# Latent attention on row halves: single banks for the maxima, denominators in a score bank, four query buffers, every engine in source order

## The chip, the cores and the metric

The kernel runs on one core of a Trainium2 chip. A core has five engines with a queue each: TensorE (PE, matmuls, with its weight loads shown as PEld), VectorE (DVE), ScalarE (ACT), GpSimd (POOL) and SyncE (SP), which issues most DMAs here. TensorE writes into PSUM, eight banks of 128 partitions by 512 fp32 words; the engines work otherwise on SBUF, which DMAs fill from and empty to HBM. The metric is the time of one execution on the device in microseconds (us); lower is better.

## The reference, cut to what matters

Two layers over 1024 latent tokens and 256 context tokens of width 1024: windowed grouped attention first, then multi-head latent attention, then a final RMSNorm. The change lies in the second layer.

```python
def latent_attention(hx, hc, w_in, q_norm, w_uq, kv_norm, w_ukv, w_out, cos, sin, need_ctx):
    scale = (B_NOPE + B_ROPE) ** -0.5                     # 64 + 32
    def project(h):
        cq, ckv, kr, g = jnp.split(h @ w_in, ...)
        q = (rms_norm(cq, q_norm) @ w_uq).reshape(b, n, B_HEADS, B_NOPE + B_ROPE)
        kv = (rms_norm(ckv, kv_norm) @ w_ukv).reshape(b, n, B_HEADS, B_NOPE + B_V)
        return q[..., :B_NOPE], q[..., B_NOPE:], kv[..., :B_NOPE], kr, kv[..., B_NOPE:], g
    ...
    def attend(qn, qr, kn, kr, v):
        s = (jnp.einsum("bqhd,bkhd->bhqk", qn, kn)
             + jnp.einsum("bqhd,bkd->bhqk", qr, kr)).astype(F32) * scale
        p = jax.nn.softmax(s, axis=-1).astype(v.dtype)
        return jnp.einsum("bhqk,bkhd->bqhd", p, v)
    ...
    yx = (ox * jax.nn.silu(gx)) @ w_out
...
x = x + gate_x[:, None] * yx
return rms_norm(x, final_g)
```

16 heads, 1024 queries, 1280 keys (context and latent), fp32 throughout.

## The kernel before

**Numbers and layout.** Matmul operands are split into a high part and a rest (`split`, L119: ScalarE copies the high part, another engine subtracts for the low part); `mm3` (L124) makes three matmuls of such pairs. Everything lives in two hand-laid arenas of SBUF, `R` (matmul operands) and `F` (fp32), addressed in KB per partition, and in the eight banks of `PB`.

**Units.** Attention runs over 16 units (`UnitB`): unit i is a pair of heads (i // 2) and a half of the queries (i % 2, 512 of them). The two heads of a pair lie in the two halves of the partitions, so their matmuls come in pairs on 64 rows each ("row halves"). Scores are computed with keys on partitions and queries on the free axis, in ten chunks of 128 keys. A softmax needs the maximum of each query first; since keys lie on partitions, the maxima are taken in a pass of their own with queries on partitions (`top`), from the high parts alone, and enter the scores as extra rows of the query operand.

**One unit.** In the loop over the ten chunks (L1491), `score(c)` makes ten matmuls into a bank pair (2 and 3, or 4 and 5), ScalarE takes the exponential of both banks into a buffer of a ring of six (`Er`, L1340), and POOL adds it to the denominators (L1343, L1345). Behind each score comes one piece of the next unit's maxima, `top(PIECES[c])`: four matmuls (or eight of half the size) into banks 0 and 1, and one reduce by VectorE over both (L1311, L1313). At c == 5 come the previous unit's denominators (`fin2`: matmuls with ones into bank 7, `fin3`: reciprocals in the bank, products) and the first five chunks of PV, which add up in bank 6; at the end the other five. Then `shift` reduces the pieces' maxima, transposes them on TensorE into bank 7 (L1318), and VectorE (L1320) and ScalarE (four small activations, L1327) write them into the next unit's query operand. Behind it stands filler work for later units: `make_K` (the keys of the next pair, in units 0, 2, ..., 12) or `make_V` (values of the next four heads, in units 3, 7, 11), through banks 0, 1 and 7.

**Buffers.** Queries have three buffers (`qbufs`): one for unit 0, two that alternate. `prep` loads a unit's queries by five DMAs. The normalised result of a unit is stored to `og_d`.

**Around it.** Ahead of the units, unit 0's maxima are interleaved with the last four gate tiles (`g_tile`). The output weights are loaded and split in 16 pieces (`wo_pieces`) that the unit loop takes one by one. Behind the units `out_tiles` multiplies eight tiles of 128 tokens with the output weights: at the top of its loop a tile's operand is split, then 48 matmuls in two halves, for each half VectorE multiplies by the gate and adds the residual (L1428, L1429) and ScalarE squares (L1430); POOL makes the norm's factor in three small steps (L1444 to L1446), and VectorE multiplies (L1457).

**What sets the order.** Inside `tc.manual_schedule(...)` the named engines keep the order of the source. Before, only TensorE is named (L1472); the other engines' queues, SP's DMAs included, are ordered by the framework's scheduler, which may bring later work forward. An engine works its queue strictly from the front.

## Time and profile before

| | us |
|---|---|
| median of 3 runs | 1663.95 (1663.37 to 1664.39) |
| the profiled execution, its own time | 1665.06 |
| its span | 1663.2 |

| engine | busy us | share |
|---|---|---|
| TensorE | 1565.0 | 94% |
| VectorE | 969.3 | 58% |
| POOL | 767.0 | 46% |
| ScalarE | 727.4 | 44% |

The attention units run from about 1004 to 1568 us of the span, the output stage from there to the end. A row of the timeline gives start, length, engine, line, operation, output and inputs, how many instructions are merged, and in brackets how long the engine stood idle before and what ended that. A row of the chain of waits gives start, length and what the end of the program waited for at that time. A row of windows gives for each engine the busy time and number of instructions in that stretch, then the granted TensorE clock, the DMA share and GB/s. A row by source line gives shortest, median and longest instruction in ns, and the start of the first and of the last.

### The profile page before, as it was taken

What the parts mean: (1) busy time and instruction counts of PE and PEld (TensorE: products, weight loads), DVE (VectorE), ACT (ScalarE), POOL (GpSimd) and SP (SyncE); (2) the same over time, 40 slices, a digit from 0 to 9 for tenths busy, and PEclk for the clock granted to TensorE, in tenths of its full rate; (3) what the DMA queues carried; (4) which work ended last, traced back from release to release, by engine and by line L of the source; (5) the groups of instructions that cost most, each with busy time, mean ns of one, the idle gap of its engine ahead of it and who ended that gap; (6) DMA issues with size and microseconds to landing.
All of it is one profiled execution on the core that took longest, in us unless ns stands there. A gap on an engine that the chain in (4) does not pass through costs nothing.

```text
span 1663.2 us, 24529 instructions
## 1 busy us (share of the span) xinstructions
PE 1565.0 (94%) x9026; PEld 1176.9 (71%) x9026; DVE 969.3 (58%) x1734; ACT 727.4 (44%) x1412; POOL 767.0 (46%) x711
## 2 busy tenths in 40 slices
PE   7899999989999999989999997999999999999898
PEld 3788888777888888879878884556555555655487
DVE  2676689547777777777251035544565456555354
ACT  3511222258777777775224214333434343333321
POOL 2653265235453334444174203655566557566500
PEclk8899999999999999999999998999999999999899
DMA  8445553663343222263048324011111111131141
GB/s 306 146 133 172 190 168 124 198 177 112 97 139 93 89 90 89 64 198 103 23 160 293 107 65 141 20 51 35 42 40 44 53 40 35 48 99 36 57 158 64
DMA packets 123697, 178.90 MB, mean 108 GB/s; under 512 B 11692, under 2 KB 71724, under 8 KB 123576
## 3 DMA queue, kind: packets, MB, share of 16 engines
q1 hardware_dynamic: 116296, 166.40, 31.6%
q10 hardware_dynamic: 7280, 10.92, 2.1%
q8 instruction: 71, 1.16, 0.3%
q14 instruction: 50, 0.41, 0.1%
HBM read 131.13 MB, written 46.15 MB: 107 GB/s over the span
## 4 chain that ended last, share of the span: by engine, by line
PE 72%; DVE 13%; issue 4%; ACT 4%; POOL 3%; DMA 3%; SPq 0%; POOLq 0%; DVEq 0%; ACTq 0%
PE PB L126 13%; PE PB L127 12%; PE PB L128 12%; DVE krF L1311 9%; PE PB L1352 8%; PE PB L1305 7%; PE PB L570 5%; PE PB L560 4%; PE PB L1338 3%; PE PB L533 2%; PE PB L534 2%; PE PB L1363 1%; ACT arena_r L1327 1%; DVE arena_f L344 1%; PE PB L674 1%
## 5 line engine op out<-in xcount | busy, mean ns | idle before, releaser
L126 PE MATMUL PB<-arena_r 128*128 128x512 f32 (+2 forms) x1312 | 479.3, 366 | 13.4 <-ACT arena_r L1327 9.3
L127 PE MATMUL PB<-arena_r 128*128 128x512 f32 (+2 forms) x1312 | 472.3, 360 | 3.1 <-POOL arena_r L727 2.2
L128 PE MATMUL PB<-arena_r 128*128 128x512 f32 (+2 forms) x1312 | 471.8, 360 | 0.2 <-DVE arena_r L122 0.2
L1345 POOL TENSOR_TENSOR arena_f<-arena_f 128x1024 f32<-128x1024 f32 x128 | 305.0, 2383 | 81.1 <-ACT arena_f L1340 72.7
L126 PEld LDWEIGHTS PB<-arena_r 128*128 128x128 f32 x1312 | 252.3, 192 | 60.5 <-ACT arena_r L1327 11.1
L127 PEld LDWEIGHTS PB<-arena_r 128*128 128x128 f32 x1312 | 252.2, 192 | 38.1 <-POOL arena_r L727 2.7
L128 PEld LDWEIGHTS PB<-arena_r 128*128 128x128 f32 x1312 | 251.9, 192 | 35.9 <-DVE arena_r L122 0.4
L1340 ACT ACTIVATE arena_f<-PB 128x1024 f32<-128x1024 f32 x160 | 164.1, 1026 | 226.0 <-PE PB L1338 222.8
L1311 DVE TENSOR_REDUCE krF<-PB 128x2 f32<-128x1024 f32 x132 | 158.9, 1209 | 127.1 <-PE PB L1305 126.9
L1338 PE MATMUL PB<-arena_r 64*128 64x512 f32 (+1 forms) x1600 | 222.4, 400 | 9.1 <-ACT arena_f L1340 5.5
L122 DVE TENSOR_TENSOR arena_r<-PB,arena_r 128x512 fp32r<-128x512 f32 (+2 forms) x215 | 140.4, 664 | 98.1 <-ACT arena_r L121 97.2
L1338 PEld LDWEIGHTS PB<-arena_r 64*128 64x128 f32 (+1 forms) x1600 | 153.6, 187 | 59.3 <-issue 14.1
L122 POOL TENSOR_TENSOR arena_r<-arena_f,arena_r 128x512 fp32r<-128x512 f32 x80 | 111.5, 1408 | 166.3 <-ACT arena_r L121 164.9
L540 DVE CUSTOM_DVE_ANT_0 arena_f<-PB,arena_f,small 128x256 f32<-128x256 f32 (+1 forms) x288 | 145.5, 524 | 32.3 <-PE PB L534 25.7
L121 ACT CAST arena_r<-PB 128x512 fp32r<-128x512 f32 (+2 forms) x215 | 120.3, 564 | 66.6 <-PE PB L560 39.6
L1352 PE MATMUL PB<-arena_f 128*64 128x512 f32 x640 | 147.3, 607 | 0.0
L1305 PE MATMUL PB<-arena_r 64*128 64x512 f32 (+1 forms) x768 | 116.8, 391 | 29.1 <-DVE krF L1311 25.5
L541 ACT ACTIVATE arena_f<-arena_f,small 128x640 f32<-128x640 f32 (+2 forms) x160 | 118.9, 744 | 27.8 <-DVE small L540 26.9
L570 PE MATMUL PB<-arena_r 128*128 128x512 f32 x336 | 120.7, 435 | 4.7 <-ACT arena_f L581 4.1
L1305 PEld LDWEIGHTS PB<-arena_r 64*128 64x128 f32 x768 | 61.3, 187 | 84.4 <-DVE krF L1311 71.6
L344 DVE SCALAR_TENSOR_TENSOR arena_f<-arena_f,small 128x512 f32<-128x512 f32 x98 | 116.3, 1232 | 4.8 <-DMA arena_f<-ada_w 4.5
L1343 POOL TENSOR_TENSOR arena_f<-arena_f 128x1024 f32<-128x1024 f32 x16 | 38.2, 2390 | 168.9 <-ACT arena_f L1340 128.2
(162 smaller groups left out, 1878.4 us busy)
## 6 DMA issues: line engine op xcount, KB each, us to landing
arena_r<-q_d SPq DMA_DIRECT2D x148, 128.0 KB, 2.8
arena_f<-ada_w SPq DMA_DIRECT2D x64, 256.0 KB, 3.3
arena_f<-a_w_in SPq DMA_DIRECT2D x40, 256.0 KB, 3.1
arena_f<-ada_w SPq DMA_DIRECT2D x16, 512.0 KB, 7.2
arena_f<-x SPq DMA_DIRECT2D x16, 512.0 KB, 4.4
q_d<-arena_f SPq DMA_DIRECT2D x16, 512.0 KB, 3.0
qn_d<-arena_f SPq DMA_DIRECT2D x16, 512.0 KB, 5.7
arena_r<-qn_d SPq DMA_DIRECT2D x16, 512.0 KB, 5.0
```

The source lines that it names most:

```text
L122: (lo_eng or nc.vector).tensor_sub(lo, src, hi.bitcast(F32))
L126: nc.tensor.matmul(o, ah, bh, start=first, stop=False)
L127: nc.tensor.matmul(o, al, bh, start=False, stop=False)
L128: nc.tensor.matmul(o, ah, bl, start=False, stop=last)
L540: nc.vector.tensor_tensor_reduce(o, S, mk, -A_SCALE, prev, ALU.add, ALU.min, mx)
L570: nc.tensor.matmul(self.pv, V[:, self.chunks[ci], self.g, :], PT[:, s], start=ci == 0 and s == 0, stop=ci == self.m - 1 and s == 1,)
L1305: nc.tensor.matmul(PB[:, bank + e, o : o + n], self.q[r, s, bs], k[r, 0, n0 : n0 + n], start=s == 0, stop=s == 2)
L1311: nc.vector.reduce_max(self.mxp[:, :, b, i], src, AX.X)
L1338: nc.tensor.matmul(PB[:, b + e, :], k[r, s, cs], q[r, sq], start=i == 0, stop=i == 4)
L1340: nc.scalar.activation(E, PB[:, b : b + 2, :], AF.Exp)
L1345: nc.gpsimd.tensor_add(acc, acc, E)
L1352: nc.tensor.matmul(PB[r, 6, :], Vq[:, c, h, :], E[:, e], start=c == 0, stop=c == NT - 1)
```

## The change

The maxima go through three banks (0, 1, 2) that are taken in turn; each piece takes two of them, one per head, and each bank has a reduce of its own. The score pairs move to banks 3 and 4, and 5 and 6; PV adds up in bank 7. The transposed maxima and the denominators go to bank 5 (`psd`), one of the score banks; ScalarE copies the denominators to SBUF (over the sums that they were made from), and the reciprocals run there. The fillers use banks 0 to 2. `shift` is cut into `turn` (reduce and transpose) and `shift` (the writes, with the engine for each half named), and `fin3` into `fin3` and `fin4`. Queries have four buffers: one each for unit 0 and unit 1, two that alternate. Output-weight splits have their low part on POOL; in the last unit VectorE makes the additions after the fifth chunk. A small exponential is put ahead of the first unit. Every engine now keeps the order of the source, and the calls in the source are moved accordingly. `out_tiles` itself is not changed.

```diff
-    qbufs = [r_at(o, 4, 512) for o in (10, 32, 40)]
+    qbufs = [r_at(o, 4, 512) for o in (10, 48, 32, 40)]
...
-    fillb = Banks(0, 1, 7)
+    fillb = Banks(0, 1, 2)
+    topb = Banks(0, 1, 2)
+    psd = PB[:, 5, :]
...
-    WoB = [r_at(o, 2, 1024) for o in (48, 56, 80, 88, 96, 104, 64, 72)]
+    WoB = [r_at(o, 2, 1024) for o in (56, 80, 88, 96, 104, 48, 64, 72)]
...
-            self.q = qbufs[0 if i == 0 else 1 + (i - 1) % 2]
+            self.q = qbufs[i if i < 2 else 2 + i % 2]
...
-        def top(self, piece, bank=0):
+        def top(self, piece, banks=None):
+            banks = banks or (topb(), topb())
...
-            src = PB[:, bank : bank + 2, 0 : n * len(piece)]
-            if len(piece) == 1:
-                nc.vector.reduce_max(self.mxp[:, :, b, i], src, AX.X)
-            else:
-                nc.vector.reduce_max(self.mxp[:, :, b : b + 2, i], src.rearrange("p e (b n) -> p e b n", b=2), AX.X)
-
-        def shift(self):
+            for e, bank in enumerate(banks):
+                if len(piece) == 1:
+                    nc.vector.reduce_max(self.mxp[:, e, b : b + 1, i], bank[:, 0:n], AX.X)
+                else:
+                    nc.vector.reduce_max(self.mxp[:, e, b : b + 2, i], shp(bank, 2, 256), AX.X)
+
+        def turn(self):
             nc.vector.reduce_max(shp(self.mx, 2, 64)[:, :, 32:36], self.mxp, AX.X, negate=True)
-            pm = PB[:, 7, 0:128]
-            nc.tensor.transpose(pm[0:100], self.mx[:, 0:100], ident)
...
+            nc.tensor.transpose(psd[0:100, 0:128], self.mx[:, 0:100], ident)
+
+        def shift(self, engs):
+            for r, eng in zip((slice(32, 36), slice(96, 100)), engs):
...
-            b = 2 + 2 * (c % 2)
+            b = 3 + 2 * (c % 2)
...
+            eng = nc.vector if self.i == NU - 1 and c > 4 else nc.gpsimd
             if c == 1:
-                nc.gpsimd.tensor_add(acc, self.E[0], E)
+                eng.tensor_add(acc, self.E[0], E)
...
             for e, r in enumerate(HALF):
-                nc.tensor.matmul(PB[r, 7, :], ones, acc[:, e], start=True, stop=True)
+                nc.tensor.matmul(psd[r, :], ones, acc[:, e], start=True, stop=True)
+            self.rec = self.acc[:, 0:512]
+            nc.scalar.copy(self.rec, psd)
 
         def fin3(self, j):
             js = slice(256 * j, 256 * j + 256)
-            nc.vector.reciprocal(PB[:, 7, js], PB[:, 7, js])
-            nc.vector.tensor_mul(self.o[:, js], self.o[:, js], PB[:, 7, js])
-            if j:
-                nc.vector.tensor_mul(self.o, self.o, self.gt.bitcast(F32))
-                load(out=og_d[self.pair, :, self.ts], in_=self.o)
+            nc.vector.reciprocal(self.rec[:, js], self.rec[:, js])
+            nc.vector.tensor_mul(self.o[:, js], self.o[:, js], self.rec[:, js])
+
+        def fin4(self):
+            nc.vector.tensor_mul(self.o, self.o, self.gt.bitcast(F32))
+            load(out=og_d[self.pair, :, self.ts], in_=self.o)
...
-                split(WoB[k][:, 0, cs], WoB[k][:, 1, cs], st)
+                split(WoB[k][:, 0, cs], WoB[k][:, 1, cs], st, nc.gpsimd)
...
-    in_order = tc.manual_schedule(engines={mybir.EngineType.PE})
+    in_order = tc.manual_schedule()
...
-            units[0].top([(b, i)], 2 * i)
-        for _ in gs[b]:
-            pass
-    units[1].prep()
-    units[0].shift()
+            units[0].top([(b, i)], (PB[:, 2 * i, :], PB[:, 2 * i + 1, :]))
+        next(gs[b])
+        next(gs[b])
+        if b == 3:
+            units[0].turn()
+            units[0].shift((nc.vector, nc.vector))
+        next(gs[b])
+        if b == 1:
+            units[1].prep()
+    nc.scalar.activation(const[:, 1:2], const[:, 1:2], AF.Exp)
...
-        if nu and ui:
-            nu.prep()
+        nnu = units[ui + 2] if ui + 2 < NU else None
         for c in range(NT):
             if c == 5:
                 if pu:
                     pu.fin2()
+                u.PV(0, 5)
+                if pu:
                     pu.fin3(0)
-                    if nu is None:
-                        pu.fin3(1)
-                u.PV(0, 5)
+                if pu and nu is None:
+                    pu.fin3(1)
+                    pu.fin4()
...
-            if 0 < ui < 12 and (c == 3 or c == 8 and ui == 6) or ui in (12, 13) and c in (3, 8):
+            if 0 < ui < 12 and c == 2 or ui == 6 and c == 7 or ui in (12, 13) and c in (2, 7):
                 next(wo_fill, None)
...
+        if nnu:
+            nnu.prep()
         if nu is None:
-            out_fill = out_tiles(fetch_out(0))
-        if pu and nu:
-            pu.fin3(1)
+            nxt = fetch_out(0)
         u.PV(5, NT)
-        u.fin()
         if nu:
-            nu.shift()
+            nu.turn()
+            if pu:
+                pu.fin3(1)
+            nu.shift((nc.vector, nc.scalar))
+            if pu:
+                pu.fin4()
             fill = make_K(u.pair + 1) if u.half == 0 and u.pair < 7 else iter(())
...
+        u.fin()
+    out_fill = out_tiles(nxt)
+    next(out_fill)
     next(out_fill)
     next(out_fill)
     units[-1].fin2()
     units[-1].fin3(0)
     units[-1].fin3(1)
+    units[-1].fin4()
```

More of the change, by code (lines that the diff above doesn't have):

```diff
@@ L1309, in top @@
[L1309 to L1327 removed]
+            b, i = piece[0]
```

36 lines of the change are left out of this document (16 added, 20 removed).

## The prediction

> **What bounds the kernel now.** I read the page first, then the last-ended chain of waits inside one attention unit, then the timeline around the stretches where TensorE stands still, and last the output stage.
>
> ```profile
> span 1663.2 us, 24529 instructions
> PE 1565.0 (94%) x9026; PEld 1176.9 (71%) x9026; DVE 969.3 (58%) x1734; ACT 727.4 (44%) x1412; POOL 767.0 (46%) x711
> PE 72%; DVE 13%; issue 4%; ACT 4%; POOL 3%; DMA 3%; SPq 0%; POOLq 0%; DVEq 0%; ACTq 0%
> ```
>
> TensorE carries 72% of the chain, VectorE 13%. VectorE's share comes from the attention units, where the chain alternates:
>
> ```profile
> 1281.34 1.24 DVE krF L1311
> ...
> 1282.62 0.75 PE PB L1305 x4
> ...
> 1284.68 0.75 PE PB L1305 x4
> ```
>
> ```profile
> 1281.14 1.31 PE L1338 MATMUL PB<-arena_r 64*128 64x512 f32 x10
> L1338 PE MATMUL PB<-arena_r x1600: 383/390/792, 1004.7 to 1560.8; 64*128 64x512 f32 x141, 36*128 36x512 f32 x37
> L1311 DVE TENSOR_REDUCE krF<-PB x132: 682/1226/1227, 976.0 to 1528.6; 128x2 f32<-128x1024 f32 x128, 128x2 f32<-128x512 f32 x4
> ```
>
> Each chunk of a unit runs a score (ten matmuls, L1338) and a maximum piece of the next unit (four matmuls, L1305, into banks 0 and 1) that one reduce over both banks empties (L1311). The next piece waits for that reduce. Pieces start at 1282.62 and 1284.68, a period of 2.06 us: 0.75 for the piece, 1.24 for the reduce, and gaps. What TensorE would need alone: ten score matmuls last 1.31 us with 0.39 for the last one, so a pair (the two row halves run together) takes (1.31 - 0.39) / 4 = 0.23; seven pairs are 1.61 us. So 0.45 us of each chunk is the reduce, not TensorE. That is the first bound.
>
> The second lies in the units' length. The transpose L1318 marks their boundaries:
>
> ```profile
> L1318 PE MATMUL PB<-ident,krF x16: 316/317/318, 1004.5 to 1535.0; 128*100 128x128 f32 x16
> 1365.71 0.32 PE L1318 MATMUL PB<-ident,krF 128*100 128x128 f32 x1
> 1396.88 0.32 PE L1318 MATMUL PB<-ident,krF 128*100 128x128 f32 x1
> 1430.58 0.32 PE L1318 MATMUL PB<-ident,krF 128*100 128x128 f32 x1
> 1467.95 0.32 PE L1318 MATMUL PB<-ident,krF 128*100 128x128 f32 x1
> ```
>
> Fifteen unit periods last 1535.0 - 1004.5 = 530.5 us. Three that nothing else disturbs are 31.17 (no filler), 33.70 (with a key filler L1263 behind the transpose) and 37.37 (with a value filler). Four, seven and three such periods would make 472.7 us, so with unit 0 in the place of one more, some 27 us are lost to disturbances:
>
> ```profile
> 1004.48 0.32 PE L1318 MATMUL PB<-ident,krF 128*100 128x128 f32 x1 [1.09 <-ACT arena_f L1146]
> 1017.96 5.74 DVE L122 TENSOR_TENSOR arena_r<-arena_f,arena_r 128x512 fp32r<-128x512 f32 x3
> 1024.88 1.22 PE L1305 MATMUL PB<-arena_r 64*128 64x256 f32 x8 [4.99 <-DVE krF L1311]
> 1048.87 0.50 PE L126 MATMUL PB<-arena_r 128*128 128x512 f32 x1 [1.93 <-ACT arena_r L1327]
> 1049.90:1053.30 3.40, 3.40 (x10) 2.61 (x9) 0.69 (x1) 0.59 (x1) 0.00 (x0) 0.51 0.00 0
> ```
>
> Unit 0 waits 4.99 us for a reduce behind output-weight splits that VectorE was given early; the filler at 1048.87 stands 1.93 us because bank 7 holds the transposed maxima until ScalarE's L1327 has read them, and the next 3.4 us run at a granted clock of 0.51.
>
> **The change part by part.**
>
> *Single banks for maxima.* A piece takes two of three banks in turn, with one reduce each. The trace has reduces of 512 columns at 0.68 us (the minimum of L1311; 1.23 for 1024), so two cost 1.36 in place of 1.23, 0.13 us more per chunk on VectorE. The first matmul of a piece needs the second reduce of the piece before last, and the second matmul needs the first reduce of the last piece. That one ends 0.62 (two pairs with their tail) + 0.05 + 0.68 = 1.35 us after its piece began; TensorE comes back after 1.61. So the chunk falls to 1.61 and VectorE, at 1.36 of it, is not the bound, by a margin of 0.26. Four of five chunks in a block were held, two blocks a unit: 8 x 0.45 = 3.6, and the last held piece of each block lasts 0.62 in place of the 0.75 quoted: 3.8 us per unit. Bounds: 2.8 if 0.1 of each wait stays, 4.1 if a pair takes 0.225.
>
> *Denominators in bank 5, fillers in banks 0 to 2.* The filler no longer shares a bank with the transposed maxima, so the 1.93 us and its slow clock go. The clean periods only lose the 3.8: 27.4, 29.9 and 33.6. (The key filler is 18 matmuls, 12 x 0.23 + 6 x 0.12 = 3.5 us, but its period is only 2.53 longer; the other 0.95 is the shift of the new maxima, for which a unit without filler waits and still will.) Copying the denominators out (L1368, as long as the copy L1356 of that shape, 0.58 below) and the reciprocal (1.76 below) lie beside the 4.46 us of PV matmuls; without that cover they would cost at least 2.3 a unit.
>
> *Unit 0 and the output weights.* The splits go to one per unit, low part on POOL, and unit 1's query has a buffer of its own, loaded two gate tiles earlier. Unit 0 becomes a clean unit without denominators: 27.4 - 1.0 for these, - 0.95 (its shift is hidden), + 1.4 for six gate matmuls moved behind its transpose: 26.8. The transpose itself comes 1.4 + 1.09 (the idle quoted) = 2.5 us earlier. POOL gets one split more a unit, half the size of an addition, beside nine additions of 2.4 us (7.27 for three, below): 23 us of 27.4, and the six exponential buffers cover its lag inside a unit.
>
> The fifteen periods: 4 x 27.4 + 7 x 29.9 + 3 x 33.6 + 26.8 = 446.5, against 530.5: **-84.0**, and -2.5 ahead of them.
>
> *Last unit.* Today the scheduler puts the first output tile's splits into ScalarE's queue amid the exponentials, and they wait for a load:
>
> ```profile
> 1537.22 5.72 PE L1338 MATMUL PB<-arena_r 36*128 36x512 f32 x41 [0.58 <-ACT arena_r L1327]
> 1542.88 1.08 PE L1363 MATMUL PB<-arena_f,small 128*64 128x512 f32 x4
> 1543.79 4.46 PE L1352 MATMUL PB<-arena_f 128*64 128x512 f32 x20
> ...
> 1556.92 1.04 ACT L121 CAST arena_r<-arena_r 128x1024 fp32r<-128x1024 f32 x1 [5.01 <-DMA arena_r<-og_d]
> 1557.99 1.22 DVE L122 TENSOR_TENSOR arena_r<-arena_r 128x1024 fp32r<-128x1024 f32 x1 [7.60 <-ACT arena_r L121]
> 1558.94 2.50 PE L1338 MATMUL PB<-arena_r 64*128 64x512 f32 x10 [5.53 <-ACT arena_f L1340]
> 1558.90:1565.40 6.50, 6.46 (x20) 2.72 (x22) 2.81 (x2) 3.00 (x3) 6.22 (x3) 0.50 0.52 148
> 1567.77 0.50 PE L126 MATMUL PB<-arena_r 128*128 128x512 f32 x1
> 1567.89 0.58 ACT L1356 COPY arena_f<-PB 128x512 f32<-128x512 f32 x1 [5.33 <-PE PB L1352]
> ```
>
> From 1542.88 to the first output matmul at 1567.77 are 24.9 us. In source order: 0.9 + 4.5, five chunks at (5.72 - 0.39) / 4.1 = 1.3 for 6.5, PV 4.5, then, in series, ScalarE's copy 0.58, its split 1.04 and VectorE's half 1.22 with gaps: 19.4. The stop of 3 us before the tile brings a slow clock, 1.7 to 3.4 us of half speed lost; I take 2.0. **-3.5** (bounds -5.5 and -2).
>
> *The output stage, in source order.* This is the part that costs. Today it is full:
>
> ```profile
> 1570.00:1600.00 30.00, 30.00 (x133) 23.92 (x132) 16.90 (x21) 5.73 (x12) 1.97 (x6) 1.00 0.36 114
> 1573.62 0.69 DVE L1428 TENSOR_TENSOR arena_f<-PB,arena_r 128x512 f32<-128x512 f32 x1 [11.08 <-PE PB L128]
> 1574.35 0.69 DVE L1429 TENSOR_TENSOR arena_f<-arena_f,arena_r 128x512 f32<-128x512 f32 x1
> 1574.95 1.76 DVE L1367 RECIPROCAL PB<-PB 128x256 f32<-128x256 f32 x1
> 1575.13 0.63 ACT L1430 ACTIVATE arena_f<-arena_f 128x512 bf16<-128x512 f32 x1 [6.66 <-DVE arena_f L1429]
> 1575.67 0.18 ACT L1430 ACTIVATION_READ_ACCUMULATOR arena_f<-arena_f 128x1 f32 x1
> ...
> 1579.53 0.69 DVE L1370 TENSOR_TENSOR arena_f<-arena_f,arena_r 128x512 f32<-128x512 f32 x1
> ```
>
> ```profile
> 1593.44 0.29 POOL L1444 TENSOR_TENSOR small<-small 128x1 f32<-128x1 f32 x1 [8.23 <-ACT arena_f L1430]
> ...
> 1594.09 0.55 POOL L1446 TENSOR_TENSOR small<-small 128x1 f32<-128x1 f32 x1
> 1594.68 1.41 DVE L1457 SCALAR_TENSOR_TENSOR arena_f<-arena_f,small 128x512 f32<-128x512 f32 x2 [1.00 <-POOL small L1446]
> ```
>
> because the scheduler splits tile n+1 while tile n multiplies. The source splits a tile at the top of its own loop, behind everything of the tile before; the compiled order of the changed kernel has on ScalarE both squares of a tile and then the cast of the next, and on VectorE the two final multiplies (L1463) and then the low half. At each of seven boundaries TensorE, done with tile n, waits for: VectorE's multiply and add (1573.62 to 1575.04) 1.42 and 0.1 before it, the square with its accumulator to 1575.85, 0.81; POOL's three small steps 1593.44 to 1594.64, 1.20, and 0.1; the two final multiplies 1.41; the low half 1.22 of which 0.08 overlaps; gaps 0.1. Sum 6.3 us; the high half (1.04) fits beside POOL. After stops of 5 to 6 us the trace shows half speed (granted clock 0.50) for 6.5 us of work at 1558.90; after the shorter 1.93 for 3.4 us. I take 5.2, which loses 2.6 (bounds 0 and 3.3). At the first boundary the last unit's denominators (1574.95 to 1580.22, 5.3 us of VectorE) stand ahead of the tile's own multiply. Counted from the tile's first half, twelve matmuls 2.75, the denominator matmuls 1.08 and the copy 0.58 let them begin at 4.5 and end at 9.8; the second half ends at 6.6, so 3.1 more. Together 7 x (6.3 + 2.6) + 3.1 = **+65.4** (bounds +47 and +70).
>
> *VectorE against POOL.* Where a denominator product read PSUM, it now reads two SBUF operands (L1373).
>
> ```profile
> 1542.58 7.27 POOL L1345 TENSOR_TENSOR arena_f<-arena_f 128x1024 f32<-128x1024 f32 x3
> 1548.57 1.83 DVE L1370 TENSOR_TENSOR arena_f<-arena_f,arena_r 128x512 f32<-128x512 f32 x1
> ```
>
> The one final product of today that met a running POOL addition took 1.83 us in place of 0.69: it ended 0.55 us after that addition. In the new order the second half's product stands ahead of the shift. It is asked for some 3.5 us into the PV block (reduces 1.36, reciprocal 1.76, small steps), the shift 4.46 + 0.3 into it, so a wait of up to 0.9 is hidden; a whole addition, 2.4, would delay the shift 1.5. With any phase as likely as any other that is a mean of 0.47 for 14 units, 6.6 us; a chain of additions that begins with the sixth exponential ends one about when the product is asked for, so I take +3 (bounds 0 and 14 x 1.5 = +21). [...]
>
> **Sum**: -2.5 - 84.0 - 3.5 + 65.4 + 3.0 = -21.6 us. The profiled execution took 1665.06 for a span of 1663.2 and was 1.1 above the median of the runs, 1663.95; the sum off the median gives 1642.3. Anything that moves the kernel before 974 us I take as zero within 2 us.
>
> **The rivals.**
>
> *A: the output stage keeps its overlap.* Then the 65.4 falls away save the 3.1: 1580. For it speaks only that a full stage is what the page shows now; against it the order of the two queues. 7%.
>
> *B: the maxima still hold the chunk.* If a piece waited for both reduces of the last one (0.62 + 0.05 + 0.60 + 0.68 + 0.04 = 1.99 us), the chunk would stay near 2.0 and 120 chunks would each give back 0.38 us: 46 us, 1688, slower than before. It decides from a chunk of about 1.8 us, where 22 us are given back. Against it: three banks leave each matmul only the older reduce. 11%.
>
> *C: the lock term is paid in full.* VectorE's product waits a whole POOL addition ahead of each shift, and the longer stop at the unit's end (1.93 us was enough for one slow stretch) costs clock in the five units without filler, 5 x 1.7: 1642.3 + 18 + 8.5 = 1669, a little slower than before. For it: POOL adds without a break there. Against it: the phase. 9%.
>
> *Main*: 73%, with an own range of 1622 to 1659 (chunks +-8, clock in the output stage -18 and +5, lock +10).
>
> **How the numbers follow.** The point is the main case, 1642.3. The 80% range takes in the main range and C: 1615 to 1669. What a measurement of this kernel can tell from no change is about 0.2%, 3.3 us: faster means below 1660.6. Main is faster in nearly all of its range (70 of 73), A always, C in 1 of 9: 0.78. Within 0.2%: 2 of main, 3 of C: 0.05. Slower: B, 5 of C and 1 of main: 0.17.
>
> **What would show it.** Right: transposes 27 to 28 us apart in units without filler; L1305 waiting for L1311 no more; slow clock gone between 1009 and 1160; in the output stage seven TensorE stops of about 6 us ended by VectorE's L122, each followed by half-speed matmuls, the first one longer. Wrong: a chunk of 1.8 us or more, stops of less than 4 us in the output stage, or L1373 lasting over 2 us in most units with the shift late behind it.

## The result, and the profile after

| | kernel before | changed kernel |
|---|---|---|
| median, measured together | 1663.66 us | 1641.47 us (1639.62 to 1646.49) |
| ratio | | 0.9873 [0.985, 0.9896] |
| span of the profiled execution | 1663.2 us | 1639.5 us |
| the fifteen unit periods | 530.5 us | 451.2 us |
| first output matmul to the end of the span | 95.5 us | 158.6 us |

The changed kernel is faster by 22.2 us, 1.3%; the interval of the ratio lies below 1. The forecast was 1642.3 with a range of 1615 to 1669. The page of the changed kernel: span, busy times, shares of the chain of waits, and the groups of the output matmuls with TensorE's idle time before them.

```profile
span 1639.5 us, 24729 instructions
...
PE 1541.3 (94%) x9026; PEld 1196.6 (73%) x9026; DVE 1008.0 (61%) x1886; ACT 733.7 (45%) x1425; POOL 776.3 (47%) x722
...
PE 79%; DVE 6%; issue 5%; POOL 4%; ACT 3%; DMA 2%; POOLq 0%; DVEq 0%; SPq 0%; ACTq 0%
...
L126 PE MATMUL PB<-arena_r 128*128 128x512 f32 (+2 forms) x1312 | 484.0, 369 | 30.8 <-ACT arena_r L121 27.6
L127 PE MATMUL PB<-arena_r 128*128 128x512 f32 (+2 forms) x1312 | 478.0, 365 | 18.7 <-DVE arena_r L122 15.6
```

VectorE's share of the chain fell from 13% to 6%: no piece waits for a reduce any more. In their place stand waits of the output tiles for their own split: TensorE's idle time is 30.8 us ahead of L126, most of it until ScalarE's half is done, and 18.7 ahead of L127, most of it until VectorE's half is done. In the kernel before these two were 13.4 and 3.1.

The timeline of the changed kernel in a block of a unit:

```profile
1281.04 0.63 PE L1305 MATMUL PB<-arena_r 64*128 64x512 f32 x4
1281.71 1.29 DVE L1311 TENSOR_REDUCE krF<-PB 128x1 f32<-128x512 f32 x2 [0.33 <-PE PB L1305]
...
1282.65 0.63 PE L1305 MATMUL PB<-arena_r 64*128 64x512 f32 x4
```

Pieces start at 1281.04 and 1282.65, so a chunk takes 1.61 us, and now VectorE waits for the pieces (0.33), not the pieces for VectorE. The transposes that mark the units, first their group (count, shortest, median and longest in ns, first and last start), then three of them on the timeline:

```profile
L1317 PE MATMUL PB<-ident,krF x16: 270/317/317, 1003.6 to 1454.8; 128*100 128x128 f32 x16
```

```profile
1030.67 0.32 PE L1317 MATMUL PB<-ident,krF 128*100 128x128 f32 x1
...
1060.70 0.32 PE L1317 MATMUL PB<-ident,krF 128*100 128x128 f32 x1
...
1088.38 0.32 PE L1317 MATMUL PB<-ident,krF 128*100 128x128 f32 x1
```

A unit with a key filler takes 30.03 us (1030.67 to 1060.70), one without filler 27.68 (to 1088.38), and by the same view one with a value filler 33.75, in place of 33.70, 31.17 and 37.37. From the first transpose to the last there are 451.2 us.

The output stage, a boundary between two tiles on the timeline:

```profile
1534.72 0.39 PE L128 MATMUL PB<-arena_r 128*128 128x512 f32 x1
1535.14 0.69 DVE L1434 TENSOR_TENSOR arena_f<-PB,arena_r 128x512 f32<-128x512 f32 x1 [4.02 <-PE PB L128]
...
1536.65 0.63 ACT L1436 ACTIVATE arena_f<-arena_f 128x512 bf16<-128x512 f32 x1 [4.71 <-DVE arena_f L1435]
...
1537.28 1.03 ACT L121 CAST arena_r<-arena_r 128x1024 fp32r<-128x1024 f32 x1
...
1538.01 0.55 POOL L1452 TENSOR_TENSOR small<-small 128x1 f32<-128x1 f32 x1
1538.36 0.50 PE L126 MATMUL PB<-arena_r 128*128 128x512 f32 x1 [3.26 <-ACT arena_r L121]
1538.59 1.41 DVE L1463 SCALAR_TENSOR_TENSOR arena_f<-arena_f,small 128x512 f32<-128x512 f32 x2 [2.03 <-POOL small L1452]
1539.92 1.22 DVE L122 TENSOR_TENSOR arena_r<-arena_r 128x1024 fp32r<-128x1024 f32 x1
1541.20 0.79 PE L127 MATMUL PB<-arena_r 128*128 128x512 f32 x1 [2.33 <-DVE arena_r L122]
```

This is the chain that the prediction wrote out, step behind step: multiply, add, square, POOL's three small steps (the last one shown), two final multiplies, low half. ScalarE's cast ends early enough for one matmul at 1538.36; the second waits for VectorE until 1541.20. From the last matmul's end (1535.11) to there are 6.09 us, of which one matmul's pitch of 0.23 is work: 5.86. The matmul that follows lasts 0.79 in place of 0.50, at a granted clock of 0.50. The first boundary is longer, since the last unit's denominators stand ahead on VectorE:

```profile
1494.25 1.74 DVE L1372 RECIPROCAL arena_f<-arena_f 128x256 f32<-128x256 f32 x1
...
1500.31 0.79 PE L126 MATMUL PB<-arena_r 128*128 128x512 f32 x1 [5.91 <-ACT arena_r L121]
...
1503.14 0.79 PE L127 MATMUL PB<-arena_r 128*128 128x512 f32 x1 [2.04 <-DVE arena_r L122]
```

The same view by stretches (window, its length, busy time and count by engine, PEclk the granted clock, DMA share and GB/s): the time from each tile's second matmul to the end of the slow clock, with what follows the first.

```profile
1503.10:1508.70 5.60, 5.56 (x13) 4.40 (x14) 0.00 (x0) 0.00 (x0) 0.00 (x0) 0.50 0.70 220
1508.70:1516.70 8.00, 8.00 (x35) 6.24 (x34) 1.38 (x2) 0.72 (x2) 0.00 (x0) 1.00 0.01 2
1522.70:1525.70 3.00, 2.92 (x7) 2.34 (x8) 0.03 (x1) 0.00 (x0) 0.00 (x0) 0.50 0.95 268
...
1541.20:1546.20 5.00, 5.00 (x12) 3.94 (x13) 0.00 (x0) 0.00 (x0) 0.00 (x0) 0.50 0.79 240
1560.60:1566.70 6.10, 6.10 (x14) 4.78 (x15) 0.00 (x0) 0.00 (x0) 0.00 (x0) 0.50 0.66 199
1580.40:1583.80 3.40, 3.34 (x8) 2.66 (x9) 0.01 (x1) 0.00 (x0) 0.00 (x0) 0.50 0.95 230
1599.00:1604.20 5.20, 5.14 (x12) 4.08 (x13) 0.01 (x1) 0.00 (x0) 0.00 (x0) 0.50 0.75 241
1618.50:1624.70 6.20, 6.18 (x15) 4.83 (x16) 0.00 (x0) 0.00 (x0) 0.00 (x0) 0.50 0.08 28
```

In the seven stretches at a clock of 0.50 TensorE works 34.2 us (5.56 + 2.92 + 5.00 + 6.10 + 3.34 + 5.14 + 6.18), at half speed, and so loses 17.1.

### The profile page after: what moved, and what is told of

Same layout as the page of the kernel before. It is cut to its first block, busy times and chain, and to the rows that moved or that the text cites. A ratio compares the mean times of both kernels' runs of the same rounds, so it can differ in the third digit from the quotient of the medians.

```text
span 1639.5 us, 24729 instructions
## 1 busy us (share of the span) xinstructions
PE 1541.3 (94%) x9026; PEld 1196.6 (73%) x9026; DVE 1008.0 (61%) x1886; ACT 733.7 (45%) x1425; POOL 776.3 (47%) x722
## 4 chain that ended last, share of the span: by engine, by line
PE 79%; DVE 6%; issue 5%; POOL 4%; ACT 3%; DMA 2%; POOLq 0%; DVEq 0%; SPq 0%; ACTq 0%
PE PB L127 13%; PE PB L126 13%; PE PB L128 13%; PE PB L1340 11%; PE PB L1355 8%; PE PB L570 5%; PE PB L1305 5%; PE PB L560 4%; PE PB L533 2%; PE PB L534 2%; DVE arena_r L122 1%; PE PB L1366 1%; DVE arena_f L344 1%; PE PB L674 1%; POOL arena_r L122 1%
## 5 line engine op out<-in xcount | busy, mean ns | idle before, releaser
L126 PE MATMUL PB<-arena_r 128*128 128x512 f32 (+2 forms) x1312 | 484.0, 369 | 30.8 <-ACT arena_r L121 27.6
L127 PE MATMUL PB<-arena_r 128*128 128x512 f32 (+2 forms) x1312 | 478.0, 365 | 18.7 <-DVE arena_r L122 15.6
L128 PE MATMUL PB<-arena_r 128*128 128x512 f32 (+2 forms) x1312 | 475.9, 363 | 0.2 <-DVE arena_r L122 0.2
L126 PEld LDWEIGHTS PB<-arena_r 128*128 128x128 f32 x1312 | 255.0, 194 | 80.7 <-ACT arena_r L121 32.0
L1348 POOL TENSOR_TENSOR arena_f<-arena_f 128x1024 f32<-128x1024 f32 x123 | 294.5, 2395 | 25.6 <-ACT arena_f L1342 18.4
L127 PEld LDWEIGHTS PB<-arena_r 128*128 128x128 f32 x1312 | 254.2, 194 | 58.0 <-DVE arena_r L122 19.1
L1311 DVE TENSOR_REDUCE krF<-PB 128x1 f32<-128x512 f32 (+1 forms) x264 | 167.3, 678 | 109.1 <-PE PB L1305 109.1
L1340 PE MATMUL PB<-arena_r 64*128 64x512 f32 (+1 forms) x1600 | 220.6, 394 | 3.9 <-ACT arena_r L1329 3.2
L122 POOL TENSOR_TENSOR arena_r<-arena_f,arena_r 128x512 fp32r<-128x512 f32 x96 | 132.2, 1389 | 166.6 <-ACT arena_r L121 157.6
L1355 PE MATMUL PB<-arena_f 128*64 128x512 f32 x640 | 143.6, 595 | 0.0
L1305 PE MATMUL PB<-arena_r 64*128 64x512 f32 (+1 forms) x768 | 107.9, 357 | 0.9 <-DVE arena_r L122 0.9
L560 PE MATMUL PB<-ident,arena_f 128*128 128x128 f32 x672 | 105.7, 274 | 0.4 <-ACT arena_f L541 0.3
L1355 PEld LDWEIGHTS PB<-arena_f 128*64 128x64 f32 x640 | 44.4, 137 | 84.2 <-issue 82.0
```

Of the source, the lines that this page charges most:

```text
L122: (lo_eng or nc.vector).tensor_sub(lo, src, hi.bitcast(F32))
L126: nc.tensor.matmul(o, ah, bh, start=first, stop=False)
L127: nc.tensor.matmul(o, al, bh, start=False, stop=False)
L128: nc.tensor.matmul(o, ah, bl, start=False, stop=last)
L560: nc.tensor.transpose(pt[:, h, :], self.Ps[h][:, ci * 128 : ci * 128 + 128], ident)
L1305: nc.tensor.matmul(bank[:, o : o + n], self.q[r, s, bs], k[r, 0, n0 : n0 + n], start=s == 0, stop=s == 2)
```

## The experiments

Times are medians; "before" is the kernel before, timed beside each experiment. All edits are made to the changed kernel, except where another is named. In the diffs, "..." stands for lines left out.

**Splitting a tile ahead (e1_cut_ahead).**

```diff
+    def cut_out(o):
+        og = shp(ogr1.next(), 2, 8, 128)
+        split(og[:, 0], og[:, 1], o.bitcast(F32))
+        return og
...
+        og_n = cut_out(nxt[0])
         for ti in range(8):
...
-            o, xi = nxt
+            og, xi = og_n, nxt[1]
...
-            og = shp(ogr1.next(), 2, 8, 128)
-            split(og[:, 0], og[:, 1], o.bitcast(F32))
...
-                    if c == 0 and ti < 7 and ti != 3:
+                    if c == 0 and ti < 7:
                         nxt = fetch_out(ti + 1)
...
+                if c == 0 and ti < 7:
+                    og_n = cut_out(nxt[0])
```

> The changed kernel, but each output tile's split (ScalarE's high half, VectorE's low half) is written one tile early in the source, behind the first half's square of the tile before, and tile 4's loads are issued like the others'. The first tile's split stays where it is. Theory (order of the source at the output boundaries): in the changed kernel's profile TensorE's seven boundaries cost 43.7 us beyond a matmul's pitch (8.5 and six times 5.86), and half speed behind them some 14 us more (a tile's 47 records last 12.3 to 13.8 us in place of 10.9). Both go: 1641.5 - 58 = 1583, within 4, stops of 2 us or more in the output stage: none behind the first tile, granted clock 0.99 or more there. Rival 1, the slow clock has a cause of its own (the stage's power or load, not the stops): only the 44 go, about 1597, granted clock still near 0.80. Rival 2, the tiles wait for their loads or for the banks anyway: above 1625.

Measured: 1594.38 against 1665.67 before, ratio 0.9582 [0.9564, 0.96]. That is 47 us less than the changed kernel, not 58. SyncE, ScalarE and TensorE in this kernel's timeline show why:

```profile
1501.26 1.70 SPq L1468 DMA_DIRECT2D out<-arena_f  x2
1503.04 0.39 SPq L1406 DMA_DIRECT2D arena_r<-og_d  x1
...
1507.81 1.04 ACT L121 CAST arena_r<-arena_r 128x1024 fp32r<-128x1024 f32 x1 [3.81 <-DMA arena_r<-og_d]
...
1508.91 0.80 PE L126 MATMUL PB<-arena_r 128*128 128x512 f32 x1 [3.73 <-ACT arena_r L121]
```

The load of tile 2 (L1406) stands behind tile 0's stores (L1468) on SyncE's queue, those wait for the final multiplies, and ScalarE then waits 3.81 us for the load. So the boundary chain was the cost, but not all of it went: a queue in source order handed part of it to the next tile's load. That the total sits near the first rival's 1597 does not speak for it: the slow clock that is left stands behind such stops (0.50 from 1508.9 to 1512.5), as the next two runs show.

**Loads two tiles ahead as well, and the first tile's loads and split ahead of the last PV block (e5_fetch_two_ahead).**

```diff
+    def out_tiles(got):
+        og_n = cut_out(got[0][0])
+        yield
...
-                    if c == 0 and ti < 7 and ti != 3:
-                        nxt = fetch_out(ti + 1)
+                    if c == 0 and ti < 6:
+                        got.append(fetch_out(ti + 2))
...
-            nxt = fetch_out(0)
+            out_fill = out_tiles([fetch_out(0), fetch_out(1)])
+            next(out_fill)
         u.PV(5, NT)
```

> The changed kernel with each output tile's split a tile ahead (as in e1_cut_ahead) and, besides, each tile's loads two tiles ahead and the first tile's loads and split written before the last unit's second PV block. What is to be told apart: e1_cut_ahead came to 1594, not 1583; its profile has the loads of tile 2 issued at 1503.04, behind the stores of tile 0 on SyncE's queue, landing when ScalarE had waited 3.81 us for them, a TensorE stop of 3.73 and half speed behind it, and the later tiles' splits still so late that each lost 0.76. Theory (what is left are loads queued behind stores): with the loads two tiles ahead the stops and the half speed behind the first tile go, 1594.4 - 10 to 13, and 2 more for the first tile's split beside PV: 1579 to 1583, clock in the output stage at least 0.99. Rival (the slow clock or the low half's 1.2 us stays as each tile's own price): 1590 to 1594.

Measured: 1577.12 against 1661.49 before, ratio 0.9489 [0.9473, 0.9505]: 17 less than e1_cut_ahead, and the fastest kernel of this study. Its output stage by stretches:

```profile
1482.30:1579.30 97.00, 89.34 (x414) 73.42 (x412) 47.84 (x67) 20.14 (x44) 7.08 (x22) 0.98 0.36 119
```

97.0 us at a mean clock of 0.98 (the expectation said 0.99), where the changed kernel has 158.6. Together with e1_cut_ahead this accounts for the whole of the loss in the output stage: with the splits and loads written in the right places, the output stage takes about as long in source order as with the scheduler (95.5 before).

**Keeping TensorE busy in its stops (e7_warm).** The waits stay; matmuls that nobody reads fill them.

```diff
+            if ti:
+                warm(24 if ti == 1 else 13)    # matmuls into bank 4
...
+                        if ti and c == 0 and k == 0:
+                            warm(8)
```

> The changed kernel with matmuls that nobody reads (into bank 4) in TensorE's output stops: 24 at the first boundary, 13 at the others, and 8 behind the first matmul of each tile, at most as long as the stops themselves (13 x 0.23 = 3.0 of 3.26, 8 x 0.23 = 1.8 of 2.04); the waits stay. Theory (half speed follows from the stops): in the changed kernel's profile TensorE works at half speed for 0.8 + 5.6, 2.9, 5.0, 6.1, 3.2, 5.1 and 6.2 us behind the seven stops, half of it lost, 17 us; with TensorE kept at work the clock is full: 1641.5 - 17 = 1624, within 4, the first low-half waits of the tiles as before. Rival 1, the slow clock in the output stage has another cause: 1641 within 4, clock near 0.80. Rival 2, the added matmuls come on top (they wait themselves or run slow): above 1646.

Measured: 1625.64, ratio 0.9784 [0.977, 0.9799], 15.8 less than the changed kernel.

```profile
1484.80:1616.00 131.20, 125.39 (x557) 99.20 (x555) 45.58 (x62) 18.52 (x40) 6.52 (x21) 1.00 0.24 79
```

The granted clock is 1.00 through the stage, where the changed kernel has 0.81 (1482.2 to 1632.7). So half speed follows from the stops here and costs 16 to 17 us of the 62; the rivals of e1_cut_ahead, e5_fetch_two_ahead and this run by which the slow clock has another cause fall.

**Two banks instead of three (e2_two_banks).**

```diff
-    topb = Banks(0, 1, 2)
+    topb = Banks(0, 1)
```

> The changed kernel with the maxima in turn over banks 0 and 1 alone, still one reduce per bank; nothing else differs. Theory (the third bank is what lets a piece begin before both reduces of the last one are done): each bank comes back only after its own reduce, the second one ends 0.62 + 0.05 + 0.68 + 0.68 = 2.0 us after the piece began, so the held chunk goes from 1.61 back to 2.0: eight held chunks in each of 14 or 15 units, 0.38 each, some 43 to 46 us, about 1686. Rival 1, one reduce per bank is enough, since the first bank comes back after 1.3 us and the row halves need not start together: the chunk stays within 0.1 of 1.61, below 1653. Rival 2, in between (a pair whose halves no longer run together costs TensorE more than a wait): above 1695.

Measured: 1681.51 against 1665.67 before, ratio 1.0098 [1.0076, 1.012]. A chunk of its timeline, and what the line of the pieces waited for (us, times):

```profile
1289.47 1.11 PE L1305 MATMUL PB<-arena_r 64*128 64x512 f32 x4
...
1291.33 0.40 PE L1305 MATMUL PB<-arena_r 64*128 64x512 f32 x1
```

```profile
  DVE krF L1311: 49.3, 120
```

The held chunk is about 1.87 us (1.86 between these two pieces), the periods add up to 491.0, 39.8 more than with three banks, and the whole change would have been 1% slower than the kernel before. The theory holds, its size was a little high: 2.0 was expected. One reduce per bank alone is worth 2.06 - 1.87 = 0.19 a chunk, the third bank the other 0.26. The units lengthen by 2.6 to 3.2 us, more than eight held chunks of 0.26 (2.1); where the rest lies was not followed.

**Order against structure (e3_new_pe_order, e4_old_all_order).** The changed kernel with only TensorE in source order, and the kernel before with every engine in it.

```diff
-    in_order = tc.manual_schedule()
+    in_order = tc.manual_schedule(engines={mybir.EngineType.PE})
```

> The changed kernel with only TensorE in the order of the source from unit 0 on, the other engines placed by the scheduler as before the change; nothing else differs. Theory (the order of ScalarE and VectorE alone makes the output stage longer, 62 us of it by the two profiles): the output stage falls back to about 95 us, and the scheduler puts output weights' splits and final multiplies among the units' work again, which cost the kernel before some 27 us of disturbed periods, a part of which comes back: 1580 to 1605. Rival 1, the order is what keeps the units at their clean periods and all 27 us and more come back: 1606 to 1630. Rival 2, the output stage is longer for another cause (banks, buffers): still about 155 us, total 1641 or more.

> The kernel before with all engines in the order of the source from unit 0 on; nothing else differs (two banks with one reduce, three query buffers, denominators in bank 7). Theory (order and banks are two independent parts): the output stage gains some 62 us, the last unit loses some 4, the periods lose part of the 27 us of disturbances (unit 0's 5 us among them) and keep the chunk of 2.06: 1663.7 + 62 - 4 - 5 to 25, so 1697 to 1717. Rival 1, the source of before is written for the scheduler, and in plain order its units stall as well (final multiplies and output-weight splits ahead of the reduces on VectorE): above 1720. Rival 2, order is not what lengthens the output stage: below 1670.

| | only TensorE in source order | every engine |
|---|---|---|
| kernel before: time; periods; output stage | 1663.66; 530.5; 95.5 | 1776.86; 585.6; 159.5 |
| changed kernel | 1595.09; 465.0; 95.7 | 1641.47; 451.2; 158.6 |

The ratio to the kernel before is 0.9582 [0.9566, 0.9598] for e3_new_pe_order and 1.0682 [1.0658, 1.0706] for e4_old_all_order. The stretches of e3_new_pe_order: unit 0, the other fourteen periods, the output stage.

```profile
1001.20:1042.90 41.70, 32.52 (x197) 20.56 (x196) 14.45 (x23) 16.32 (x20) 32.29 (x18) 0.84 0.39 114
1042.90:1466.20 423.30, 419.87 (x3011) 279.69 (x3009) 277.35 (x399) 198.62 (x266) 305.38 (x133) 1.00 0.18 53
1497.90:1593.60 95.70, 88.85 (x414) 73.49 (x412) 45.78 (x66) 19.89 (x43) 7.67 (x22) 0.98 0.29 97
```

Whatever the structure, source order adds 63 to 64 us in the output stage. What it brings to the changed kernel is unit 0: 41.7 us with the scheduler and 27.06 without, 14.6 (with the scheduler, ScalarE's split of an output weight stands ahead of an exponential and waits 6.51 us for its load, and the mean clock is 0.84); and 5.6 between the last transpose and the output stage (31.7 against 26.1). The other fourteen periods are 423.3 against 424.2: what cleared the disturbed ones was the rest of the change (banks, buffers, splits on POOL, moved calls; these were not tried one by one), not the order. So with the source as it is, the change without source order on the other engines is the faster kernel, by 46 us. The old structure in source order lost 55 us in its periods as well. That is the time of e4_old_all_order's first rival, but only in part its cause: the transposes do wait about 1.0 us each for a reduce behind the gate multiply, yet the larger wait is another. TensorE stood 48.2 us, in 14 waits ahead of the maxima, for a query load that SyncE issues behind the store of finished heads; before the change there were two such waits, 5.9 us together. The next run tests that in the changed kernel.

**Queries loaded where the kernel before loads them (e8_late_query).**

```diff
+        if nu and ui:
+            nu.prep()
         for c in range(NT):
...
-        if nnu:
-            nnu.prep()
```

> The changed kernel with each unit's query loaded where the kernel before has it, at the start of the unit before it, and not ahead of the second PV block one unit earlier still; the buffers stay. Theory (in the order of the source a query load stands on SyncE's queue behind the store of finished heads, which waits for VectorE's gate multiply, and then takes some 6 us to land, as in e4_old_all_order, where each unit's first maxima waited 4.5 us for it): 14 units, 4.5 to 5.5 each: 1641.5 + 63 to 77 = 1705 to 1718. Rival (the load is hidden by the shift and the fillers in most units): less than 20 us, below 1662.

Measured: 1743.33 against 1661.49 before, ratio 1.0492 [1.0471, 1.0513]: 101.9 us more than the changed kernel, more than expected. SyncE's queue and TensorE at the start of a unit:

```profile
1098.47 0.34 SPq L1377 DMA_DIRECT2D og_d<-arena_f  x1
...
1099.38 0.53 SPq L1290 DMA_DIRECT2D arena_r<-qn_d  x1
...
1105.86 2.25 PE L1305 MATMUL PB<-arena_r 64*128 64x512 f32 x4 [5.10 <-DMA arena_r<-qn_d]
1107.35 2.89 PE L1340 MATMUL PB<-arena_r 64*128 64x512 f32 x10
```

The store L1377 leaves SyncE when VectorE's gate multiply has ended (1098.44), the query load L1290 behind it, and the first piece waits 5.10 us. In the changed kernel the load stands some 8 us ahead of that store (1083.11 and 1091.25). The score behind the wait lasts 2.89 for ten matmuls in place of 1.31: the stop brings half speed (granted clock 0.50 from 1105.9 to 1110.2), which the expectation had left out. The loss falls on 13 periods, 4.1 to 10.5 us each: the fourteenth moved load, in unit 1, has no store ahead of it yet, and its period is still 30.03.

**VectorE's products beside POOL's additions (e9_no_adds, e6_shift_first).** The first kernel leaves out all but one of the additions of each unit, and adds 1 to each denominator, so these are not those of a softmax; in the second, VectorE's half of the shift comes ahead of the second half's reciprocal and product.

```diff
-            elif c:
-                eng.tensor_add(acc, acc, E)
...
-            nc.scalar.copy(self.rec, psd)
+            nc.scalar.activation(self.rec, psd, AF.Copy, bias=1.0)
```

> The changed kernel without the additions of the exponentials behind the first two of each unit (POOL's, and VectorE's in the last unit), and with 1 added to each denominator; VectorE's queue is otherwise as it was. Theory (a VectorE product of two SBUF operands waits for the end of a POOL addition): in the changed kernel's profile the second-half product lasts 1.15 to 2.29 us and the gate multiply 1.66 to 2.06, against 0.42 and 0.69 in the output stage, where POOL adds nothing; the three periods in which the product ended 1 us later than in the others are the three longer ones (30.82, 30.44, 28.45). Without the additions every product lasts 0.43 and every gate multiply 0.69, and those three periods fall to their like: periods together 449.2 in place of 451.2. Rival 1 (each unit pays some of it, up to the 18 us of the third case): periods together below 445. Rival 2 (the longer products have another cause, such as the loads that write SBUF): durations as before, periods 451.

```diff
             nu.turn()
-            if pu:
-                pu.fin3(1)
             nu.shift((nc.vector, nc.scalar))
             if pu:
+                pu.fin3(1)
                 pu.fin4()
```

> The changed kernel with VectorE's half of the shift ahead of the second half's reciprocal and product (not between product and gate multiply); nothing else differs. Theory (a product that meets a running POOL addition delays the shift in few units only): in the changed kernel's profile three periods are longer than their like, 30.82 and 30.44 for 30.03 and 28.45 for 27.68, together 2.0 us; these go, periods together 449 to 449.5 in place of 451.2, nothing else moves. Rival 1 (the wait for VectorE costs every unit some, as the last prediction's third case had it): periods together 440 or less. Rival 2 (the product and gate multiply then stand ahead of the next unit's reduces and hold the first chunks instead): periods together above 451.5.

Products in the changed kernel (the group, and one of the three late ones with the shift L1322 behind it), then the group in e9_no_adds:

```profile
L1373 DVE TENSOR_TENSOR arena_f<-arena_f x32: 424/1114/2399, 1046.3 to 1496.0; 128x256 f32<-128x256 f32 x32
```

```profile
1208.75 2.29 DVE L1373 TENSOR_TENSOR arena_f<-arena_f 128x256 f32<-128x256 f32 x1
1211.08 0.68 DVE L1322 TENSOR_TENSOR arena_r<-PB,ident 4x512 fp32r<-4x512 f32 x1
```

```profile
L1371 DVE TENSOR_TENSOR arena_f<-arena_f x32: 424/425/427, 1044.5 to 1494.0; 128x256 f32<-128x256 f32 x32
```

Without these additions all 32 products last 0.42, and the fifteen periods add up to 449.3: the three long ones (30.82, 30.44 and 28.45) become 30.10, 30.02 and 27.69. So the longer products come from the additions, and they cost 1.9 us, in three units. (The kernel took 1637.65, timed once, 3.8 less than the changed one; 1.7 of that lies ahead of the units.)

Why these three: the late products stand at the ends of units 6, 12 and 13, the only ones with a second output-weight split, at c == 7. POOL's half of that split shifts the additions behind it, so that one begins just ahead of the product at 1208.75:

```profile
1207.15 1.28 POOL L122 TENSOR_TENSOR arena_r<-arena_f,arena_r 128x512 fp32r<-128x512 f32 x1
1208.38 4.93 POOL L1348 TENSOR_TENSOR arena_f<-arena_f 128x1024 f32<-128x1024 f32 x2
```

At the ends of units 12 and 13 the same split stands at 1393.20 and 1423.65, and no other unit has it. No run moves these splits alone.

With the shift first, periods add up to 457.6 and the kernel takes 1650.63 (timed once): reciprocal, product and gate multiply then stand ahead of the reduces and hold the next pieces (units without filler 28.4 in place of 27.68, those with a key filler 30.6 to 31.1), the second rival.

**The first piece ahead of the first score (e10_piece_first)**, an edit of e5_fetch_two_ahead.

```diff
+            if nu and c == 0:
+                nu.top(PIECES[c])
             u.score(c)
-            if nu:
+            if nu and c:
                 nu.top(PIECES[c])
```

> e5_fetch_two_ahead with each unit's first maximum piece ahead of its first chunk's score on TensorE, nothing else. Theory (in a unit without key or value filler TensorE waits 0.6 us for the shift of the new maxima: the first score block lasts 9.0 us there and 7.88 elsewhere; the next unit's first piece needs no shift and lasts 0.63): seven units without filler, 0.6 each, some 3 to 4 us less than e5_fetch_two_ahead: 1573 to 1575. Rival (the piece's reduces stand behind the gate multiply on VectorE, so that the second piece waits instead): within 1 of 1577, or above it.

Measured: 1583.75, ratio 0.9522 [0.9506, 0.9538], 6.6 slower than e5_fetch_two_ahead. Three of the four units without filler fall to between 27.2 and 27.5 (from 27.7), but those with one rise: value fillers to 34.5 from 33.75, key fillers to between 30.8 and 33.6 from between 30.0 and 30.8. In a unit with a key filler the piece now stands directly behind the filler and waits 0.27 for a filler's bank (VectorE's low half of a key), and two scores follow each other behind it. The longest, 33.6, is the one behind unit 6: there this wait is 1.53 us, and 3.4 us at a clock of 0.50 follow. The expectation's "seven units without filler" was a miscount: seven have a key filler, and four of the fifteen have none. What else makes up the rise of 0.8 to 1.1 in the others was not followed.

## Why the prediction was right, and where it was not

Each step by the two profiles, in the order in which the sum was made:

| step | predicted | measured | how |
|---|---|---|---|
| ahead of the units | 0 within 2 | +1.7 | first piece 974.86 and 976.53 |
| transpose of unit 0 | -2.5 | -2.5 | 1004.48 to 1003.61, less the 1.7 |
| fifteen periods | -84.0 | -81.2 | 530.5 to 451.2, less the 1.9 of the next row |
| VectorE against POOL | +3 | +1.9 | 451.2 - 449.3, e9_no_adds |
| last unit | -3.5 | -5.6 | last transpose to first output matmul: 32.8 to 27.1 |
| output stage | +65.4 | +62.1 | the rest of the span: 95.5 to 157.6 |
| sum | -21.6 | -23.6 | the spans differ by 23.7 |

The first output matmul of the changed kernel is counted at 1481.98, one pitch of 0.23 ahead of the second, which has to wait; it started at 1480.95. The first row is scatter: in six experiments whose source is the same up to there the first piece starts between 973.3 and 978.2.

*Single banks for maxima.* Right in place and size. The clean periods gave back 3.5 to 3.7 us in place of 3.8. e2_two_banks shows that the third bank does it, and rival B is answered with it: its mechanism exists, at 1.87 us a chunk and not 1.99, where banks are two; with three, L1305 waits for L1311 nowhere. The granted clock is 1.00 from 1003.6 to 1462.8, as the prediction asked for 1009 to 1160.

*Unit 0.* The time was right (27.06 for 26.8), the reason half right. The prediction put it on the placing of the splits; e3_new_pe_order has the same source and still 41.7, so it is source order that keeps the splits where the source has them.

*Four query buffers.* This is the step that failed without showing in the sum. The prediction priced unit 1's buffer and let the loads of all other units, now two units ahead, stand at nothing. In source order their place on SyncE's queue is worth 102 us (e8_late_query). The price of nothing was right for the change as it is, because the loads did move; but the work that made it so was not named, and a reader who drops that line gets a kernel 5% slower than before.

*Last unit.* The 19.4 us in series came out at 19.2 (1462.81 to 1481.98). The 2.0 for a slow clock did not come: TensorE stopped for 1.75 us and, one matmul on, for 0.76, and the granted clock stayed at 1.00 (second row below, of windows: the third number from its end). So the step came out just beyond its bound of -5.5.

```profile
1480.95 0.50 PE L126 MATMUL PB<-arena_r 128*128 128x512 f32 x1 [1.75 <-ACT arena_r L121]
```

```profile
1462.80:1482.20 19.40, 16.82 (x97) 7.57 (x95) 13.40 (x11) 8.36 (x9) 6.85 (x3) 1.00 0.45 147
```

*Output stage.* All three parts were there: stops 43.7 (8.5 and six of 5.86; predicted 47.2), half speed 17.1 (18.2), and 1.3 besides. Each stop was priced 0.4 too long, the first one 0.9. e1_cut_ahead and e5_fetch_two_ahead take the stops away, e7_warm the slow clock alone. Rival A fell; its time was to be had, though, with the splits and loads moved in the source: e5_fetch_two_ahead came to 1577 where the rival had 1580.

*VectorE against POOL.* What the prediction calls the lock shows in the trace as products that end behind an addition: in the changed kernel 30 of the 32, all but the two in the output stage, end 0.28 us after the POOL addition that ran as they began, and 14 of the 16 gate multiplies 0.55 after one. In the kernel before, where a product reads one operand from PSUM, 16 of them met an addition and took 0.42 us all the same. e9_no_adds agrees, 0.42 us without additions against up to 2.40 with them. Rival C had every unit pay a whole addition, and no run shows its 18 us (the bound of 21 less the 3 of the sum): e9_no_adds shows 1.9 in their place. Most units pay nothing, because the shift waits for the transpose anyway: the usual product (1.15 to 1.47 us) ends ahead of it, and only the three that met an addition just begun (2.27 to 2.29 us) delay it. The prediction took the phase of POOL's additions in part as a matter of chance and set +3; by the trace it is the second output-weight split that sets it, where the prediction counted one split per unit. That its +3 is near the 1.9 is in part luck. Rival C's slow clock was absent here and came in e5_fetch_two_ahead: the last period takes 30.00 us there in place of 28.45, with 3.4 us at a clock of 0.50.

## What to carry to other kernels

Putting queues in source order makes every line of the source a scheduling decision, DMA issues included: for each moved load ask what the lines ahead of it in the queue wait for, and issue loads before stores that wait (101.9 us in e8_late_query). Where a chain of small steps on other engines stands between two tiles, write the next tile's operand preparation ahead of the present tile's epilogue, and count the slow clock behind the stop beside the stop itself (17.1 us beside 43.7 here). A reduce that holds a matmul can be met by one more bank in the ring while the reduces themselves take as long as before (1.29 us for two, and a chunk of 1.61 in place of 1.87). Source order is no gain by itself: the changed kernel took 1595 us with TensorE alone in source order, 1641 with every engine, and 1577 only once the output stage's splits and loads had been moved.

## What the runs showed of the hardware

The loss to half speed differs from 1.5 to 3.1 us for the six equal stops of 5.86. In the changed kernel's output stage the granted clock is 0.50 from 1498.44 to 1508.68, 1518.92 to 1525.74, 1539.40 to 1546.22, 1556.46 to 1566.70, 1576.94 to 1583.77, 1597.42 to 1604.25 and 1614.49 to 1624.73, and 1.00 between. These stretches last 6.83, 10.24 or 13.65 us, two, three or four times 3.41: whatever the moment at which a stop begins, the clock changed on this one grid, and what a stop costs depends on where the work restarts between two changes. What makes a stretch slow stays open. Before the change one stop of 1.93 us was followed by 3.41 us of half speed (1049.94 to 1053.36), while 1.75 us in the last unit of the changed kernel cost nothing; counted back in steps of 3.41 us from a change of the clock, each lies whole in one step (1046.53 to 1049.94, TensorE busy for 1.48 us of it, and 1477.96 to 1481.37, busy for 1.66). And two stops of 0.47 and 0.66 us behind the transpose at 1426.39 of the changed kernel left the clock at 1.00 (both in the step from 1426.76 to 1430.17, TensorE busy for 2.28 us of it), while the same two stops in e5_fetch_two_ahead, behind the transpose at 1428.03, were followed by 3.4 us at 0.50.

VectorE's gate multiply lasted 1.66 to 2.06 us beside POOL's additions, and 0.69 where POOL added nothing (twice in the changed kernel, and all 16 times in e9_no_adds): beside additions that is 2.4 to 3.0 times as long.
